# Hybrid decoder step: other tiles for the second projection part's activations

## The chip, the cores and the metric

The kernel runs on one core of a Trainium2 chip. A core has a matrix engine (TensorE, PE in the profile), three other compute engines (VectorE, DVE; ScalarE, ACT; GpSimd, POOL), a sequencer that in this kernel issues every DMA (SyncE, SP), and sixteen DMA engines that carry them. The engines run on their own, each through its instructions in a fixed order, and wait for one another through semaphores. The metric is the device time of one execution in microseconds; the median over three runs is compared.

## What is computed

The reference is one step of one layer of a decoder trunk over 1024 prompt tokens and 8 sample sequences of one token, 1032 columns in all, with 1024 channels. All of it is fp32.

```
h    = rmsnorm(x, norm_mix)
proj = h @ w_in                       # 1024 -> 3224 columns
mix  = [ S5 | mLSTM | GLA | RWKV-7 ](proj) @ w_out
x    = x + mix
h2   = rmsnorm(x, norm_ffn)
ug, uv = split(h2 @ ffn_w_up)         # 2 x 2816
x    = x + (gelu(conv3(ug)) * uv) @ ffn_w_down
y    = rmsnorm(x, norm_final)
```

The four mixers are recurrences over the tokens, 256 channels each, computed in chunks. The sample group takes one step from given states. All final states are outputs too.

## The kernel before

Activations lie transposed, channels on the 128 partitions and tokens along the free dimension, so x is eight blocks of 128 channels. The 1032 tokens are worked in two parts (`SEGS`): columns 0 to 511, and 512 to 1031 with the eight sample columns at their end (520). A matrix product in fp32 is three products in the faster fp32r form: the activation is split into a rounded part and the rest, the weight likewise, and `mm3` (L1132) adds high by high (L1139), rest by high (L1140) and high by rest (L1141) over the eight blocks. A part of 520 columns is worked as two chunks of 260, each with a PSUM buffer of its own; there are three such buffers (`g`).

The order of the program is: `win(0)`, the input projections of the first part; the first part's mixers (`SEQ0`); `win(1)`, the projections of the second part; `w_out` and `ffn` for the first part; the second part's mixers and the decoding step (`SEQ1`); `w_out` and `ffn` for the second part. That is not the order in which it runs. A planner orders each engine's instructions at build time, from its own estimates of durations: an instruction is placed when its tile is free and its inputs are there, and among those that are ready the one with the lower number goes first. `k.pr` sets these numbers: weight loads and splits (`S`) come first of all, projections, output projection and FFN (`E`) count from the same start as the mixers but have far fewer instructions ahead of them, and the matmuls of the projections (`G`) come last, so that they fill TensorE between the mixers' own.

A tile with a tag (`ga` pool, one buffer for each tag) waits until the tile before it on that tag has been read for the last time. The tags that matter here are:

- h0 to h7, 128x2x520 each: the split activations (`htile`, L1126). They are written by `split_gain` (L1189) in `win(0)`, `win(1)` and `ffn`, and by `w_out`. The last group of FFN weights also uses h0 to h3.
- xa0 to xa7: the residual x2 of the first part, from `w_out` on. Before that, xa0 holds blocks of x for `x_rstd` (L1200), xa2 a small weight and xa3 the sample columns `hd`.
- p0 to p4: gated FFN activations. Before the FFN, p0 to p2 hold every third weight (`load_w`).
- t: a ring of five tiles for everything short-lived, among it blocks of x (`load_x`, L1146), normed blocks and the evicted projections.

For `win(1)` each of the eight blocks takes this way: `load_x` brings 128x520 of x into a t tile (L1147), GpSimd multiplies it by the reciprocal norm `k.r1` into another t tile (`split_norm`, L1197), ScalarE writes the gained and rounded part into h (L1191), VectorE the rest (L1192). `k.r1` is computed earlier, by `x_rstd`, during the first part. The last projection of `win(0)` reads h0 to h7 in that order.

SyncE issues all DMAs in one queue, weight loads (L1120), x blocks (L1147), evicted projections (L1221), rows from the mixers (yD) and to them. A load that waits for its tile holds up what stands behind it.

Of the kernel before, what the change touches and what calls it, by code (L numbers as in the profile page):

```python
# [7 lines left out]
F32=mybir.dt.float32; F32R=mybir.dt.float32r; I32=mybir.dt.int32; BF16=mybir.dt.bfloat16  # L8
# [1089 lines left out]
HW=520  # L1098

W1=5  # L1100
TB=5
# [7 lines left out]
def load_w(k,src,tags=None):  # L1109

    nc=k.nc; k.wn+=1
    if tags: r=k.wp.tile([128,1024],F32,tag="wr",name="wr",bufs=k.wb[0]); h,l=[k.ga.tile([128,1024],F32R,tag=n,name=n) for n in tags]
    elif k.w3 and k.wn%3==0: r,h,l=[k.ga.tile([128,1024],t,tag=n,name=n) for n,t in (('p0',F32),('p1',F32R),('p2',F32R))]
    else: r,h,l=[k.wp.tile([128,1024],t,tag=n,name=n,bufs=b) for n,t,b in zip(('wr','wh','wl'),(F32,F32R,F32R),k.wb)]
    shp=src.shape; n=int(np.prod(shp[1:]))
    def view(t):
        v=t[:,0:n]
        return v if len(shp)==2 else v.rearrange("p (a b)->p a b",a=shp[1]) if len(shp)==3 else v.rearrange("p (c a b)->p c a b",c=shp[1],a=shp[2])
    with k.pr('S'):
        nc.sync.dma_start(out=view(r),in_=src)  # L1120
        nc.scalar.copy(h[:,0:n],r[:,0:n])  # L1121
        for c in range(0,n,256): nc.gpsimd.tensor_tensor(out=l[:,c:c+256],in0=r[:,c:c+256],in1=h[:,c:c+256].bitcast(F32),op=ALU.subtract)  # L1122
    return view(h),view(l)

def tt(k): return k.tp.tile([128,HW],F32,tag="t",name="t",bufs=k.tb)
def htile(k,i): return k.ga.tile([128,2,HW],F32R,tag="h%d"%i,name="h%d"%i)  # L1126
def gps(k,tag=None): return k.psm.tile([128,512],F32,tag=tag,name=tag,bufs=1 if tag=="mc" else 2) if tag else k.psg.tile([128,512],F32,tag="g",name="g")

def split_act(k,h,N,src):
# [13 lines left out]
def chunks(N):  # L1143
    return [(0,N)] if N<=512 else [(0,N//2),(N//2,N)]

def load_x(k,i,c0,c1):  # L1146
    t=tt(k); k.nc.sync.dma_start(out=t[:,0:c1-c0],in_=k.xT[i*128:(i+1)*128,c0:c1]); return t[:,0:c1-c0]  # L1147

class Ms:

# [38 lines left out]
def split_gain(k,N,i,x,gname):  # L1189
    h=htile(k,i); g=v1(k,gname,i)  # L1190
    k.nc.scalar.activation(out=h[:,0,0:N],in_=x,func=AF.Identity,scale=g)  # L1191
    k.nc.vector.scalar_tensor_tensor(out=h[:,1,0:N],in0=x,scalar=g,in1=h[:,0,0:N].bitcast(F32),op0=ALU.mult,op1=ALU.subtract)  # L1192
    return h

def split_norm(k,N,i,x,r,gname):

    t=tt(k)[:,0:N]; k.nc.gpsimd.tensor_tensor(out=t,in0=x,in1=r[:,0:N],op=ALU.mult)  # L1197
    return split_gain(k,N,i,t,gname)

def x_rstd(k,c0,c1):  # L1200
# [8 lines left out]
def w_in_fm(k,hr,seg,idx,w=None,tag=None):  # L1209
    nc=k.nc; c0,c1=seg; N=c1-c0; hs,r=hr  # L1210
    w=w or load_w(k,k.wfm[idx])
    dst,sc=k.fmdst[idx]
    e=tt(k); ps=[]
    for a,b in chunks(N):
        p=gps(k,tag); ps.append(p)
        mm3(k,p[:,0:b-a],w,hs,a,b)
    if r is not None: r=r.rstd()
    for (a,b),p in zip(chunks(N),ps):
        if r is None: nc.scalar.activation(out=e[:,a:b],in_=p[:,0:b-a],func=AF.Identity,scale=sc)
        else: nc.vector.scalar_tensor_tensor(out=e[:,a:b],in0=p[:,0:b-a],scalar=sc,in1=r[:,a:b],op0=ALU.mult,op1=ALU.mult)  # L1220
    nc.sync.dma_start(out=dst[:,c0:c1],in_=e[:,0:N])  # L1221
# [173 lines left out]
def build(ctx,tc,a):  # L1395
    nc=tc.nc; k=K(); k.nc=nc; k.tc=tc; k.pr=Pri(tc,PRI); tc.cur_priority=1000000
    for n in ('xT','wfm','wmv','wgv','wu','wg','wout','wup','wdn','wdl','yT'): setattr(k,n,a[n])
    k.wb=(2,2,2); k.wn=0; k.w3=True; k.tb=TB
    pool=lambda n,b=1,**kw: ctx.enter_context(tc.tile_pool(name=n,bufs=b,**kw))
    dr=pool("dr",space=DRAM)  # L1400
    D=lambda n,s: dr.tile(list(s),F32,name=n)
# [16 lines left out]
    def win(s):  # L1418
        c0,c1=SEGS[s]
        with k.pr('E'):  # L1420
            if s==0:
                m=Ms(k,c1-c0,1,"ma",2); hs=[]; xs=[]; w=[load_w(k,k.wfm[ORDER[0][1]])]
                xt=[k.mx.tile([128,n,512],F32,tag=g,name=g) for g,n in (('r_rc',4),('r_KB',2),('r_KR',2))]
                for i in range(8):
                    x=(xt[0][:,i] if i<4 else xt[1+(i-4)//2][:,i%2]); xs.append(x)
                    with k.pr('S'): nc.sync.dma_start(out=x,in_=k.xT[i*128:(i+1)*128,c0:c1])
                    if i==W1: w.append(load_w(k,k.wfm[ORDER[1][1]]))
                    hs.append(split_gain(k,c1-c0,i,xs[i],'nmix'))
                    if i==0: m.add(xs[0],True)
                for i in range(1,8): m.add(xs[i],True,nc.vector)  # L1430
                g=k.wgs=k.ga.tile([128,8,64],F32R,tag="xa2",name="wgs"); wr=k.mx.tile([128,8,24],F32,tag="r_12",name="r_12")
                nc.sync.dma_start(out=wr,in_=k.wg)
                nc.gpsimd.memset(g.rearrange("p k (u f)->p k u f",u=2)[:,:,:,24:32].bitcast(F32),0.0)
                nc.scalar.copy(g[:,:,0:24],wr)
                nc.gpsimd.tensor_tensor(out=g[:,:,32:56],in0=wr,in1=g[:,:,0:24].bitcast(F32),op=ALU.subtract)
                hr=hs,m
            else:
                w=[]; hr=[split_norm(k,c1-c0,i,load_x(k,i,c0,c1),k.r1.rstd(),'nmix') for i in range(8)],None
                m=(c1-c0)%128; k.hd=k.ga.tile([128,8,32+m],F32R,tag="xa3",name="hd")
                nc.gpsimd.memset(k.hd[:,:,m:32].bitcast(F32),0.0)  # L1440
                for i in range(8):
                    for u in range(2): nc.gpsimd.tensor_copy(k.hd[:,i,32*u:32*u+m],hr[0][i][:,u,c1-c0-m:c1-c0])
        for n,(kd,i) in enumerate(ORDER):
            with k.pr('E'):
                if kd=='fm': w_in_fm(k,hr,SEGS[s],i,w.pop(0) if w else None,{3:'mb',4:'mb',5:'mc'}.get(n) if s==0 else None)
                elif kd=='tm': w_in_tm(k,hr,SEGS[s],i)
                else: w_in_g(k,hr,SEGS[s])
                if s==0 and n==0: m.tokens()
            if s==0 and n==10: setup()
# [3 lines left out]
    def setup():  # L1453
        s5_setup(k,a['par'],a['bcv'],a['dT'],a['wglu'])
        with k.pr('E'): k.r1=x_rstd(k,*SEGS[1])
# [7 lines left out]
    def go(seq):  # L1463
        for z in seq.split(): run[z[0]](z[1:])
    win(0)
    go(SEQ0)
    win(1)
    nc.sync.dma_start(out=a['psh'],in_=rcD[:,:,1023:1024]); nc.sync.dma_start(out=a['osh'],in_=rcD[:,:,1024:1032])
    x2=[k.ga.tile([128,HW if m<2 else 512],F32,name="xa%d"%m,tag="xa%d"%m)[:,0:512] for m in range(8)]
    with k.pr('E'):  # L1470
        r=w_out(k,0,512,x2); k.w3=False; rest,end=ffn(k,0,512,x2,r)
    go(SEQ1)
    for hp in range(2):
        r=slice(hp*64,hp*64+64)
# [15 lines left out]
    x2=[xb.tile([128,HW],F32,name="xb%d"%m,tag="xb%d"%m) for m in range(8)]  # L1490
    with k.pr('E'):
        r=w_out(k,512,1032,x2,rest)
# [45 lines left out]
@with_exitstack  # L1538
def kernel(ctx: ExitStack, tc: tile.TileContext, args):
    build(ctx, tc, args)  # L1540
# [19 lines left out]
```

## Time and profile before

| what | value |
|---|---|
| median of three runs | 1469.35 us (1467.53 to 1475.34) |
| profiled execution, its own time | 1472.93 us |
| its span, first to last instruction | 1471.2 us |
| mean granted TensorE clock | 0.980 |
| PE busy | 1411.1 us, 96% of the span |
| DVE, POOL, ACT busy | 903.7, 914.8, 684.6 us |
| DMA | 179.80 MB, mean 122 GB/s |

The profile is one execution. Its page gives busy times, the span in 40 slices with the busy share in tenths, and the groups of instructions; other views give single instructions in order of time, one line's instructions, or the busy time in chosen stretches. A row such as `g<-h,wh 128*128 128x260` is a matmul that writes the PSUM tile g from h and the weight wh, with 260 columns. The bracket at the end of a row in the time line gives the idle time ahead of it and what ended that.

### The profile page before, as it was taken

The page shows a single profiled execution, that of the slowest core. Times are in us where ns is not written, and L with a number is a line of the kernel's source. Part 1 is how long each engine was busy: PE and PEld are TensorE (multiplying, and loading weights), DVE is VectorE, ACT ScalarE, POOL GpSimd, SP SyncE. Part 2 cuts the span into 40 slices and gives each one's busy share as a digit, 9 for nine tenths or more (in the row PEclk, how much of TensorE's full clock was granted, in tenths as well). Part 3 has the DMA queues.
Part 4 walks back from the last instruction along what each step waited for, and adds up shares of the span by engine and source line. Part 5 has one row for each costly group of instructions (what it writes and reads, how often), then busy time and mean ns, then how long its engine had stood idle before and what let it go on. Part 6 is the DMA issues. An engine that isn't in the chain of part 4 may idle for free.

```text
span 1471.2 us, 26807 instructions
## 1 busy us (share of the span) xinstructions
PE 1411.1 (96%) x10115; PEld 1239.2 (84%) x10115; DVE 903.7 (61%) x1979; ACT 684.6 (47%) x1151; POOL 914.8 (62%) x1154
## 2 busy tenths in 40 slices
PE   8879999999999989999899999999999999999997
PEld 6758878988999767777678778878999999999997
DVE  7988857667568956786946755455265434343434
ACT  6153454656376463766555436354443323222323
POOL 8555455546345664675754766877876757676764
PEclk9989998999999999999999999999999999999999
DMA  6455444743355523432223433353333232233332
GB/s 231 158 170 149 151 147 129 220 126 109 87 180 166 155 80 101 129 115 89 90 85 98 138 122 92 116 166 103 126 119 115 88 100 87 92 96 89 98 91 87
DMA packets 110266, 179.80 MB, mean 122 GB/s; under 512 B 33016, under 2 KB 67192, under 8 KB 110136
## 3 DMA queue, kind: packets, MB, share of 16 engines
q1 hardware_dynamic: 110136, 178.08, 39.3%
q8 instruction: 80, 1.31, 0.4%
q14 instruction: 50, 0.41, 0.1%
HBM read 148.10 MB, written 28.41 MB: 120 GB/s over the span
## 4 chain that ended last, share of the span: by engine, by line
PE 43%; DVE 4%; DMA 1%; ACT 1%; POOL 1%; issue 1%; DVEq 0%; SPq 0%; POOLq 0%; ACTq 0%
PE g L1139 14%; PE g L1141 14%; PE g L1140 13%; POOL wl L1122 1%; DVE t L1388 0%; ACT wh L1121 0%; DVE yo L1369 0%; DVE h L1192 0%; DMA DB<-d_o 0%; DMA DV<-r_KB 0%; PE g L1171 0%; DVE t L1323 0%; DVE xa L1305 0%; DMA b2a<-uD 0%; PE mb L400 0%
## 5 line engine op out<-in xcount | busy, mean ns | idle before, releaser
L1122 POOL TENSOR_TENSOR wl<-wr,wh 128x256 fp32r<-128x256 f32 x708 | 576.3, 845 | 276.5 <-ACT wh L1121 257.8
L1140 PE MATMUL g<-h,wh 128*128 128x260 f32 (+1 forms) x1536 | 493.0, 322 | 2.4 <-DVE h L1192 2.3
L1141 PE MATMUL g<-h,wl 128*128 128x260 f32 (+1 forms) x1536 | 491.9, 321 | 1.2 <-POOL wl L1122 1.2
L1139 PE MATMUL g<-h,wh 128*128 128x260 f32 (+1 forms) x1536 | 490.8, 321 | 0.2 <-ACT h L1191 0.2
L1121 ACT CAST wh<-wr 128x1024 fp32r<-128x1024 f32 x177 | 185.2, 1046 | 288.2 <-PE g L1140 146.6
L1140 PEld LDWEIGHTS g<-h,wh 128*128 128x128 f32 x1536 | 290.4, 189 | 28.6 <-DVE h L1192 5.8
L1141 PEld LDWEIGHTS g<-h,wl 128*128 128x128 f32 x1536 | 290.7, 189 | 23.9 <-POOL wl L1122 2.7
L1139 PEld LDWEIGHTS g<-h,wh 128*128 128x128 f32 x1536 | 289.4, 189 | 22.8 <-issue 0.9
L1139 PE MATMUL g<-p,wh 128*128 128x260 f32 (+1 forms) x496 | 162.6, 328 | 4.0 <-DVE xa L1305 2.3
L1141 PE MATMUL g<-p,wl 128*128 128x260 f32 (+1 forms) x496 | 162.0, 327 | 0.1
L1140 PE MATMUL g<-p,wh 128*128 128x260 f32 (+1 forms) x496 | 161.9, 327 | 0.0
L1139 PEld LDWEIGHTS g<-p,wh 128*128 128x128 f32 x496 | 94.7, 191 | 12.9 <-DVE xa L1305 2.8
L1141 PEld LDWEIGHTS g<-p,wl 128*128 128x128 f32 x496 | 94.6, 191 | 8.9 <-POOL wl L1122 0.6
L1140 PEld LDWEIGHTS g<-p,wh 128*128 128x128 f32 x496 | 94.7, 191 | 7.4 <-issue 0.2
L1122 POOL TENSOR_TENSOR p<-p,p 128x256 fp32r<-128x256 f32 x76 | 61.6, 841 | 42.9 <-ACT p L1121 34.7
L1305 DVE TENSOR_TENSOR xb<-xb,g 128x260 f32<-128x260 f32 x80 | 33.7, 424 | 60.7 <-PE g L1141 60.7
L1328 DVE TENSOR_TENSOR t<-g,r 128x260 f32<-128x260 f32 x44 | 18.6, 424 | 56.2 <-PE g L1141 51.2
L1305 DVE TENSOR_TENSOR xa<-xa,g 128x512 f32<-128x512 f32 x48 | 32.6, 681 | 32.0 <-PE g L1141 32.0
L1140 PE MATMUL g<-h,p 128*128 128x260 f32 (+1 forms) x144 | 48.9, 339 | 0.0
L1139 PE MATMUL g<-h,p 128*128 128x260 f32 (+1 forms) x144 | 48.6, 338 | 0.0
L1141 PE MATMUL g<-h,p 128*128 128x260 f32 (+1 forms) x144 | 48.6, 338 | 0.0
L1131 DVE TENSOR_TENSOR p<-t,p 128x512 fp32r<-128x512 f32 (+1 forms) x44 | 38.3, 871 | 16.1 <-ACT p L1130 15.9
(725 smaller groups left out, 2670.7 us busy)
## 6 DMA issues: line engine op xcount, KB each, us to landing
wr<-in_wup_dram SPq DMA_DIRECT2D x88, 512.0 KB
wr<-in_wfm_dram SPq DMA_DIRECT2D x27, 512.0 KB
wr<-in_wdn_dram SPq DMA_DIRECT2D x22, 512.0 KB
wr<-in_wdl_dram SPq DMA_DIRECT2D x22, 512.0 KB
wr<-in_wout_dram SPq DMA_DIRECT2D x13, 512.0 KB
p<-in_wfm_dram SPq DMA_DIRECT2D x11, 512.0 KB
t<-in_xT_dram SPq DMA_DIRECT2D x16, 260.0 KB
b4c<-B8Td SPq DMA_DIRECT2D x6, 512.0 KB
```

What stands on the lines that cost most here:

```text
L1121: nc.scalar.copy(h[:,0:n],r[:,0:n])
L1122: for c in range(0,n,256): nc.gpsimd.tensor_tensor(out=l[:,c:c+256],in0=r[:,c:c+256],in1=h[:,c:c+256].bitcast(F32),op=ALU.subtract)
L1131: k.nc.vector.tensor_tensor(out=h[:,1,0:N],in0=src,in1=h[:,0,0:N].bitcast(F32),op=ALU.subtract)
L1139: T.matmul(out,wh[:,i],a,start=i==0,stop=False)
L1140: T.matmul(out,wh[:,i],b,start=False,stop=False)
L1141: T.matmul(out,wl[:,i],a,start=False,stop=i==n-1)
L1305: V.tensor_tensor(out=x2[m][:,a:b],in0=x2[m][:,a:b],in1=p[:,0:b-a],op=ALU.add)
L1328: for (a,b),p in zip(ch,pg): V.tensor_tensor(out=g[:,2+a:2+b],in0=p[:,0:b-a],in1=r[:,a:b],op=ALU.mult)
```

## The change

`htile` takes its tag from a list, `k.home`, that the program sets ahead of each stage. In `win(0)` the list is h0 to h7 as before. For `win(1)` it is p3, p4, xa4, xa6, then h0 to h3. From then on it is h4 to h7, then h0 to h3, for the output projections and both FFN parts. `win(1)` loads its blocks of x into xa0 and xa1 in turn, and the norm is written over them, so that it takes no t tile. The last four blocks of x2 lie two by two in xa4 and xa6, which have the size of an h tile now; xa5 and xa7 are gone.

```
-def htile(k,i): return k.ga.tile([128,2,HW],F32R,tag="h%d"%i,name="h%d"%i)
+def htile(k,i): return k.ga.tile([128,2,HW],F32R,tag=k.home[i],name=k.home[i])
...
-def load_x(k,i,c0,c1):
-    t=tt(k); k.nc.sync.dma_start(out=t[:,0:c1-c0],in_=k.xT[i*128:(i+1)*128,c0:c1]); return t[:,0:c1-c0]
+def load_x(k,i,c0,c1,tag=None):
+    t=k.ga.tile([128,HW],F32,tag=tag,name="xr") if tag else tt(k)
+    k.nc.sync.dma_start(out=t[:,0:c1-c0],in_=k.xT[i*128:(i+1)*128,c0:c1]); return t[:,0:c1-c0]
...
-def split_norm(k,N,i,x,r,gname):
+def split_norm(k,N,i,x,r,gname,over=False):
-    t=tt(k)[:,0:N]; k.nc.gpsimd.tensor_tensor(out=t,in0=x,in1=r[:,0:N],op=ALU.mult)
+    t=x if over else tt(k)[:,0:N]; k.nc.gpsimd.tensor_tensor(out=t,in0=x,in1=r[:,0:N],op=ALU.mult)
...
+    k.home=['h%d'%i for i in range(8)]; k.wb=(2,2,2); k.wn=0; k.w3=True; k.tb=TB
...
-                w=[]; hr=[split_norm(k,c1-c0,i,load_x(k,i,c0,c1),k.r1.rstd(),'nmix') for i in range(8)],None
+                w=[]; hr=[split_norm(k,c1-c0,i,load_x(k,i,c0,c1,'xa%d'%(i%2)),k.r1.rstd(),'nmix',True) for i in range(8)],None
...
+    k.home=['p3','p4','xa4','xa6','h0','h1','h2','h3']
     win(1)
+    k.home=['h%d'%((i+4)%8) for i in range(8)]
...
-    x2=[k.ga.tile([128,HW if m<2 else 512],F32,name="xa%d"%m,tag="xa%d"%m)[:,0:512] for m in range(8)]
+    x2=[k.ga.tile([128,HW if m<2 else 512],F32,name="xa%d"%m,tag="xa%d"%m)[:,0:512] for m in range(4)]
+    for m in (4,6):
+        t=k.ga.tile([128,2,HW],F32,name="xa%d"%m,tag="xa%d"%m); x2+=[t[:,0,0:512],t[:,1,0:512]]
```

More of the change, by code (lines that the diff above doesn't have):

```diff
@@ L1397, in build @@
     for n in ('xT','wfm','wmv','wgv','wu','wg','wout','wup','wdn','wdl','yT'): setattr(k,n,a[n])
-    k.wb=(2,2,2); k.wn=0; k.w3=True; k.tb=TB
+    k.home=['h%d'%i for i in range(8)]; k.wb=(2,2,2); k.wn=0; k.w3=True; k.tb=TB
     pool=lambda n,b=1,**kw: ctx.enter_context(tc.tile_pool(name=n,bufs=b,**kw))
```

## The prediction

> **What bounds the kernel now.** I read the page first, then TensorE's share by stretches, then the queues of the engines around the stretch that stands out.
>
> ```profile
> span 1471.2 us, 26807 instructions
> PE 1411.1 (96%) x10115; PEld 1239.2 (84%) x10115; DVE 903.7 (61%) x1979; ACT 684.6 (47%) x1151; POOL 914.8 (62%) x1154
> PE   8879999999999989999899999999999999999997
> PEclk9989998999999999999999999999999999999999
> ```
>
> TensorE (PE) is the bound: it is busy for 96% of the span and no other engine passes 62%. All that can be won lies where it idles or runs at a reduced clock. The seventh slice, from 221 us, has PEclk at 8. The view of stretches looks into it:
>
> ```profile
> core 0: us, PE busy (x) PEld busy (x) DVE busy (x) ACT busy (x) POOL busy (x), PEclk, DMA share, GB/s
> 157.60:170.00 12.40, 12.40 (x72) 10.05 (x71) 11.35 (x29) 4.53 (x7) 8.50 (x10) 1.00 0.52 155
> 208.00:215.60 7.60, 7.60 (x39) 5.52 (x38) 2.59 (x6) 2.68 (x6) 2.19 (x4) 1.00 0.63 201
> 215.60:224.70 9.10, 4.14 (x49) 3.56 (x48) 8.02 (x14) 3.74 (x7) 6.06 (x8) 0.83 0.63 204
> 224.70:243.10 18.40, 18.40 (x144) 16.69 (x143) 17.11 (x34) 9.53 (x17) 13.62 (x23) 0.81 0.37 116
> 243.10:270.00 26.90, 26.90 (x245) 25.58 (x244) 14.29 (x37) 14.41 (x30) 11.05 (x17) 1.00 0.70 210
> ```
>
> PE is full up to 215.6 and again from 243.1. Between the two it idles 9.10-4.14 = 4.96 us, and then works 18.40 us at a mean granted clock of 0.81. The time lines of PE, POOL and SyncE's queue (SP), and the rows of the norm and the split, say what happens there:
>
> ```profile
> 208.41 0.39 PE L1139 MATMUL g<-h,wh 128*128 128x512 f32 x1
> 215.31 0.40 PE L1141 MATMUL g<-h,wl 128*128 128x512 f32 x1
> 223.73 1.11 PE L289 MATMUL ma<-r_rs,r_xa 64*64 64x64 f32 x8 [3.44 <-DVE r_rs L286]
> 224.77 0.80 PE L1139 MATMUL g<-h,wh 128*128 128x260 f32 x2
> 244.17 0.28 PE L1139 MATMUL g<-h,wh 128*128 128x260 f32 x1
> 244.29 0.28 PE L1140 MATMUL g<-h,wh 128*128 128x260 f32 x1
> L1147 SPq DMA_DIRECT2D t<-in_xT_dram x8: 327/336/464, 212.9 to 236.5; - x8
> L1197 POOL TENSOR_TENSOR t<-t,r x8: 1280/1304/1656, 219.6 to 239.2; 128x520 f32<-128x520 f32 x8
> L1191 ACT ACTIVATE h<-t,vec x8: 712/730/732, 223.7 to 240.6; 128x520 fp32r<-128x520 f32 x8
> L1192 DVE SCALAR_TENSOR_TENSOR h<-t,vec,h x8: 743/957/1628, 226.2 to 241.8; 128x520 fp32r<-128x520 f32 x8
> ```
>
> The first part's last projection reads its eight activation tiles from 208.4 to 215.7 (512 columns). The second part's eight columns of x are loaded only from 212.9, normed from 219.6, split from 223.7, and the last split starts at 241.8. Its first matmul (260 columns) is at 224.8. So the second part's operands are made after the first part has ended, and PE waits for them.
>
> **The change, part by part.** No compute instruction is added or removed: eight loads, eight norms, eight pairs of splits stay. What changes is which tile each waits for.
>
> *Tiles 0 to 3* (p3, p4, xa4, xa6) no longer wait for the first part. What they still need is r1, the second part's reciprocal norm, and a free tile for x:
>
> ```profile
> 156.95 0.64 ACT L1176 ACTIVATE r<-r 128x520 f32<-128x520 f32 x1
> L1440 POOL MEMSET hd<- x1: 292/292/292, 3.1 to 3.1; 128x192 f32 x1
> L1164 POOL TENSOR_TENSOR s<-s,xr x7: 1292/1336/2306, 35.4 to 94.8; 128x520 f32<-128x520 f32 x7
> ```
>
> r1 is there at 157.6. xa0 is free after the last sum of squares (94.8), xa1 from the start. The planner does hoist: the second part's memset, which waits for nothing, ran at 3.1 us, 210 us ahead of its neighbours in the code. So I expect four norms and split pairs from about 158 us: POOL 4 x 1.304 = 5.2, ScalarE 4 x 0.730 = 2.9, VectorE 4 x 0.957 = 3.8 us. They lie under PE's work, which has no idle time there (12.40 of 12.40); but VectorE is 11.35 of 12.40 busy, so the cover is thin. If all 3.8 us came through to PE, they would cost 3.8; if the same work, gone from 224 to 243 (VectorE 17.11 of 18.40), pays it back, nothing or a small gain. I take 0, since the total stays.
>
> *Tiles 4 to 7* (h0 to h3) come free in the order in which the last projection reads them: three matmuls of about (215.31-208.41)/23 = 0.30 us each, so from 209.3 on, one per 0.9 us. Their x sits in xa0 and xa1, normed in place. Two can wait there, normed, so tiles 4 and 5 need only ScalarE 0.73 and VectorE 0.96 and are there by about 212; VectorE is busy 2.59 of 7.60 us then. Tiles 6 and 7 need a load into the freed xa first:
>
> ```profile
> 212.91 0.46 SPq L1147 DMA_DIRECT2D t<-in_xT_dram  x1
> 219.66 0.33 SPq L1120 DMA_DIRECT2D wr<-in_wfm_dram  x1
> 227.67 9.14 SPq L1147 DMA_DIRECT2D t<-in_xT_dram  x4
> 248.56 0.33 SPq L1120 DMA_DIRECT2D wr<-in_wfm_dram  x1
> 233.32 1.31 POOL L1197 TENSOR_TENSOR t<-t,r 128x520 f32<-128x520 f32 x1 [1.66 <-DMA t<-in_xT_dram]
> ```
>
> Four loads took 9.14 us of SP's queue, 2.3 each. With one load, norm and split pair (2.3+1.3+0.7+1.0 = 5.3) tile 6 is ready near 217.5 and tile 7 near 219. By then PE has tiles 0 to 5 for the first projection's two halves: 6 x 3 x 2 = 36 matmuls, 0.12 us apart (244.17 to 244.29), 4.3 us from 215.7 to 220.0, beside the mixers' own matmuls. The bubble left is 0 by this, and 3.4 us if the load is as late as the one that held POOL at 233.3; I take 0.5.
>
> *The gain.* The idle 4.96 us go. The clock: 18.40 x (1-0.81) = 3.50 us. Sum 8.46. If the bubble left stays short, both go together; less 0.5 that is 8.0.
>
> The clock term rests on rows: 0.83 and 0.81 granted after PE's 3.44 us wait, 1.00 before and after. The Trainium skill (TensorE: Matmul & The Clock Gate, section "What's actually happening") says the clock falls to half after about one idle window of 3.4 us and comes back after as long of work; the trace agrees with its 3.44 us. By that rule a bubble of 0.5 us costs no clock, so the 3.50 goes whole or not at all.
>
> *Smaller edits.* Column 1's load into xa1 waits for nothing and may go out at the start: 260 KB, which at the 204 GB/s of the stretch quoted take 1.3 us; between 0 (a queue with room) and 1.3 (all ahead of the first operands); I take 0. The norm in place drops eight t tiles from the shared ring of five, which eases the projections' evictions: no gain counted. The last four x2 halves share xa4 and xa6, which the second part now reads to its end; x2 is written after that, so the wait is over before it starts. FFN and output projection rotate to h4 first: the same matmuls. At the very end the last weights go into h0 to h3, now the later four tiles, and so come free 12 matmuls x 0.12 = 1.4 us later, under a whole group of 8 x 2 x 12 matmuls (23 us): 0.
>
> *What is late next.* The output projection after the second part:
>
> ```profile
> 456.95 0.39 SPq L583 DMA_DIRECT2D yD<-b2a  x1
> 827.92 2.42 DMA yD<-b2a
> 466.13 2.68 SPq L1277 DMA_DIRECT2D t<-yD  x4
> 470.91 0.62 ACT L1130 CAST h<-t 128x512 fp32r<-128x512 f32 x1 [0.51 <-DMA t<-yD]
> 469.11 0.28 PE L1141 MATMUL g<-h,wl 128*128 128x260 f32 x1
> 473.20 0.48 PE L1139 MATMUL g<-h,p 128*128 128x512 f32 x1
> ```
>
> The second part would end at 469.4-8.0 = 461.4. The last mixer's rows are stored at 456.95, land 2.42 later (an equal store), and from load to first matmul pass 473.20-466.13 = 7.1: 466.4. The gap becomes 5.0 instead of 3.8 us, with mixer matmuls in it either way. That takes 0 to 1.2; I take 0, because h4 to h7 are free by then and the loads need not queue.
>
> After that nothing stands in the way of the gain: the last decoding mixer stores its rows at 976, and the second output projection's weights go out at 1002.
>
> ```profile
> 975.99 0.38 SPq L1047 DMA_DIRECT2D yD<-d_g  x1
> 1002.33 11.59 SPq L1120 DMA_DIRECT2D wr<-in_wout_dram  x3
> ```
>
> That is 26 us of slack against 8.
>
> **The sum.** The profiled execution took 1472.93 (span 1471.2 and 1.7 around it), 3.6 over the median of 1469.35, inside the runs shown. On its own time: 1472.93-8.0 = 1464.9; carried to the median, 1469.35-8.0 = 1461.4. The open costs (3.8 early splits, 2.9 more of bubble, 1.3, 1.2) do not all fall together; with about half of their 9.2, 4.6, the forecast's own range is 1457 to 1466, its lower end from the third rival's gap filled.
>
> **The rivals.**
>
> *Only the first four help.* If tiles 4 to 7 come as late as now, PE gains what tiles 0 to 3 feed: three PSUM buffers x 4 x 3 matmuls x 0.12 = 4.3 us: 1465.0. For it: two x tiles only, and loads that queue behind others on SP. Against it: tiles 4 and 5 need no load at that time.
>
> *The gain stops at the output projection.* VectorE at 92% from 157.6 to 170 gets 3.8 us more and POOL 5.2, both ahead of the mixers by the planner's priorities. If the mixers before the output projection are late by 5.2, their rows land at 464.6 and the first matmul is at 471.6 instead of 473.2: a gain of 1.6, 1467.7. Rows for it: the same split took 743 to 1628 ns, the norm 1280 to 1656. The Trainium skill (SBUF — State Buffer, section "SBUF: two separate sides") says that VectorE with two SBUF inputs and a reading GpSimd lock each other out of one port for a whole instruction; the spread agrees, and by that rule the early pairs stretch instead of fitting in. Against this rival: 224 to 243 gets lighter by the same amount.
>
> *More than forecast.* The output projection's gap of 3.8 us closes too, since its first four tiles are free early: 8.46+3.8 = 12.3, 1457.1. It needs the last mixer some 12 us earlier, and only VectorE's lighter load speaks for that.
>
> *Slower: loads that wait at SP's head.* With two x tiles, six loads wait for a split of the load two before. At 2.3 us each that is 13.7 us in which SP issues nothing else, moved from a stretch where PE had no operands into 158 to 216, where PE is full and the weights (L1120) and the mixers' loads queue behind. It decides once a wait outlasts the three weight sets held; uncovered, 13.7 plus 3.5 of clock less 8.0: 1469.35+9.2 = 1478.6. Against it: the planner places a load where it expects the tile to be free.
>
> **How the numbers follow.** Forecast 0.50, first four only 0.16, stopped at the output projection 0.08, more 0.12, slower 0.14. Changes under 0.5%, 7.3 us here, can't be told from none: faster is under 1462.0, slower over 1476.7. The forecast lies on the edge: 0.32 of its 0.50 below 1462.0. Faster: 0.32+0.12+0.03 (from the first rival) = 0.47. Slower: 0.14. Same: 0.39. The range holds all but the last rival: from 1457.1 and 1467.7 it reaches outward by 3 and 6 us, about what the runs shown lie below and above their median (1467.53 and 1475.34, 1.8 and 6.0): 1454 to 1474.
>
> **What would show it.** Right: four norms (L1197, now x<-x) near 158 to 180; first 260-column matmul within 1 us of the last 512-column one; granted clock 1.00 through 216 to 243; the second part's end near 461. Wrong: splits of tiles 4 to 7 still after 220 (first rival); y's loads waiting near 459 with PE idle behind (second); x loads of several us on SP before 208 with PE idle (slower).

## The result, and the profile after

The changed kernel takes 1495.24 us (median of 4 runs, 1489.45 to 1498.19) against 1470.32 us (median of 4, 1467.53 to 1475.34) for the kernel before on the same chip. The ratio is 1.0158 with a 95% interval of 1.0138 to 1.0178: slower by 1.6%, where 1461.4 and a gain were forecast. The profiled execution is the fastest of the four, 1489.45 us with a span of 1487.6 against 1471.2, so the traces show 16.4 us of the loss. Two executions in the experiments below lie far from all others of their kernel (1696.96 us in e10, 3120.18 us in e11); they are in the medians given there, but not in the ratios.

The page's span, its busy line for TensorE (PE) and its 40 slices, of the kernel after:

```profile
span 1487.6 us, 26798 instructions
PE 1423.3 (96%) x10115; PEld 1243.5 (84%) x10115; DVE 928.8 (62%) x1979; ACT 681.1 (46%) x1151; POOL 925.9 (62%) x1154
PE   8699999999999989999999999999999999999997
PEclk9899999999999989999999999999999999999999
```

The 8 of the clock in the slice from 221 us is gone. The five engines have the same counts of instructions as before. VectorE (DVE) is busy 25.1 us longer than before (903.7) though it does the same work. The view of stretches, at the places that the prediction read and with the columns shown there:

```profile
157.60:170.00 12.40, 12.40 (x72) 10.04 (x71) 11.60 (x20) 4.96 (x7) 11.78 (x15) 1.00 0.50 155
208.00:215.60 7.60, 7.60 (x63) 6.15 (x63) 3.57 (x4) 6.30 (x11) 7.46 (x10) 1.00 0.41 124
215.60:224.70 9.10, 9.10 (x70) 8.01 (x69) 6.71 (x9) 5.15 (x9) 8.68 (x12) 1.00 0.61 188
224.70:243.10 18.40, 18.40 (x171) 17.10 (x172) 11.88 (x35) 9.53 (x20) 6.74 (x13) 1.00 0.49 174
```

PE is busy 9.10 of 9.10 us where it idled 4.96, and the granted clock is 1.00 where it was 0.83 and 0.81. The rows of the norm (now L1198) and of VectorE's half of the split (now L1193):

```profile
L1198 POOL TENSOR_TENSOR xr<-xr,r x8: 1288/1540/1941, 160.0 to 218.5; 128x520 f32<-128x520 f32 x8
L1193 DVE SCALAR_TENSOR_TENSOR h<-xr,vec,h x4: 760/1181/1233, 212.7 to 223.5; 128x520 fp32r<-128x520 f32 x4
L1193 DVE SCALAR_TENSOR_TENSOR p<-xr,vec,p x2: 1195/1216/1237, 166.6 to 167.7; 128x520 fp32r<-128x520 f32 x2
L1193 DVE SCALAR_TENSOR_TENSOR xa<-xr,vec,xa x2: 1103/1104/1105, 174.7 to 177.8; 128x520 fp32r<-128x520 f32 x2
```

Four tiles are ready by 179, the other four by 224.7. So the tiles come early, as intended. What that cost is first seen on the chain of RWKV's first chunk. VectorE's time line, before and then after: one step of the forward substitution (L247), its end (the transpose L248), and the first of four state updates (L296).

```profile
169.99 0.21 DVE L247 TENSOR_TENSOR ma<-ma,r 128x50 f32<-128x50 f32 x1
193.25 0.66 DVE L248 STREAM_TRANSPOSE r<-ma 128x256 f32<-128x256 f32 x1
218.16 0.90 DVE L296 TENSOR_TENSOR r_S<-r_S,r 128x256 f32<-128x256 f32 x1
```

```profile
178.87 0.20 DVE L247 TENSOR_TENSOR ma<-ma,r 128x50 f32<-128x50 f32 x1
200.41 0.70 DVE L248 STREAM_TRANSPOSE r<-ma 128x256 f32<-128x256 f32 x1
230.38 0.42 DVE L296 TENSOR_TENSOR r_S<-r_S,r 128x256 f32<-128x256 f32 x1
```

The same step is 8.9 us late behind the four early splits, the substitution ends 7.2 us late, and the first state update is 12.2 us late. The other 5.0 came on between 200 and 230, and PE's time line shows a part of it. In the kernel before, around the bubble, the matmuls of one state update (L281 and L284, L289, L293):

```profile
214.42 0.39 PE L284 MATMUL ma<-r_KB,r_rc 128*64 128x64 f32 x4
215.63 0.68 PE L289 MATMUL ma<-r_rs,r_xa 64*64 64x64 f32 x8
216.95 0.71 PE L293 MATMUL ma<-r_KB,r 128*128 128x128 f32 x4 [0.64 <-DVE r_KB L290]
```

and in the kernel after, with the two parts' projections:

```profile
217.40 0.39 PE L1141 MATMUL g<-h,wl 128*128 128x512 f32 x1
217.62 0.28 PE L1139 MATMUL g<-p,wh 128*128 128x260 f32 x1
219.85 0.40 PE L284 MATMUL ma<-r_KB,r_rc 128*64 128x64 f32 x4
223.98 0.68 PE L289 MATMUL ma<-r_rs,r_xa 64*64 64x64 f32 x8
227.80 0.61 PE L293 MATMUL ma<-r_KB,r 128*128 128x128 f32 x4
```

The first 260-column matmul starts 0.22 us after the last 512-column one: no bubble. But from L284 to L293 RWKV's step now takes 7.95 us (227.80 - 219.85) instead of 2.53 (216.95 - 214.42). VectorE has a share in it: its copy behind L284 (L286) starts at 222.35, 2.1 us after L284 has ended, since L448 and L468 stand ahead of it.

The lateness goes on. The last matmul of the second part's projections (469.11 before), the first one of the output projection (473.20 before), the last mixer's rows for the output projection of the first part (SyncE's queue; 456.95 before), the y loads that follow them, and the weights of the second output projection (1002.33 before):

```profile
468.52 0.28 PE L1141 MATMUL g<-h,wl 128*128 128x260 f32 x1
469.32 0.40 PE L1139 MATMUL g<-h,p 128*128 128x512 f32 x1
472.16 0.37 SPq L583 DMA_DIRECT2D yD<-b2a  x1
475.74 2.13 SPq L1278 DMA_DIRECT2D t<-yD  x4
1017.85 0.33 SPq L1120 DMA_DIRECT2D wr<-in_wout_dram  x1
```

The second part's projections end at 468.8, 0.6 us earlier than before and not 8.0: the gain at 216 is spent by then. The output projection starts 3.9 us earlier, on the mixers that are done, but the last mixer's rows are 15.2 us late, the second weights 15.5, the span 16.4. On PE the gain at 216 is given back in small waits. Of the stretches of 50 us, two of before and the same two of after:

```profile
250.00:300.00 50.00, 50.00 (x450) 45.58 (x451) 32.30 (x67) 32.94 (x65) 25.86 (x38) 1.00 0.68 208
450.00:500.00 50.00, 49.26 (x368) 42.23 (x367) 44.59 (x103) 29.41 (x54) 27.86 (x34) 1.00 0.55 171
```

```profile
250.00:300.00 50.00, 48.04 (x436) 42.92 (x437) 28.76 (x61) 22.78 (x48) 20.68 (x35) 0.97 0.54 163
450.00:500.00 50.00, 47.23 (x308) 40.30 (x307) 38.64 (x79) 29.96 (x62) 20.19 (x31) 0.93 0.46 144
```

and four of the waits in PE's time line after (the last number is the idle time, then who ended it):

```profile
177.95 0.69 PE L400 MATMUL mb<-b4f 128*64 128x64 f32 x16 [2.39 <-DVE r L246]
290.87 0.82 PE L112 MATMUL ma<-r,lora 96*128 96x256 f32 x4 [1.96 <-DVE r L108]
372.18 1.22 PE L257 MATMUL ma<-r_KB,r_rc 32*32 32x32 f32 x32 [2.13 <-ACT r_KB L249]
477.86 0.50 PE L1139 MATMUL g<-h,p 128*128 128x512 f32 x1 [1.92 <-ACT h L1130]
```

Three of the four stand at a mixer's matmul that is late, the fourth at the output projection. Each engine works through a fixed order, so the projections' matmuls behind such an instruction can't fill the wait. In the table each pair is PE's idle time and the time lost to the clock, busy x (1 - granted clock), in us, summed from stretches of 50 us:

| stretch | before | after |
|---|---|---|
| 150 to 200 | 0.0 + 0.0 | 2.7 + 1.4 |
| 200 to 250 | 5.0 + 4.5 | 0.0 + 0.0 |
| 250 to 450 | 1.5 + 0.0 | 5.0 + 2.9 |
| 450 to 500 | 0.7 + 0.0 | 2.8 + 3.3 |
| 500 to 600 | 7.1 + 4.7 | 7.1 + 8.3 |
| 600 to 900 | 11.2 + 2.7 | 12.0 + 2.8 |

The 9.5 us between 200 and 250 are won; 20.4 are lost elsewhere. The balance is 10.9 of the 16.4 us. The other 5.5 is time in which PE counts as busy, which I can't place.

### The profile page after: what moved, and what is told of

Same layout as the page of the kernel before. It is cut to its first block, busy times and chain, and to the rows that moved or that the text cites. A ratio compares the mean times of both kernels' runs of the same rounds, so it can differ in the third digit from the quotient of the medians.

```text
span 1487.6 us, 26798 instructions
## 1 busy us (share of the span) xinstructions
PE 1423.3 (96%) x10115; PEld 1243.5 (84%) x10115; DVE 928.8 (62%) x1979; ACT 681.1 (46%) x1151; POOL 925.9 (62%) x1154
## 4 chain that ended last, share of the span: by engine, by line
PE 64%; DVE 16%; POOL 6%; ACT 5%; issue 4%; DMA 4%; SPq 0%; DVEq 0%; POOLq 0%; ACTq 0%
PE g L1140 17%; PE g L1139 17%; PE g L1141 17%; POOL wl L1122 4%; PE ma L213 1%; ACT wh L1121 1%; POOL p L1122 1%; DMA yD<-b2a 1%; POOL s L1165 1%; PE g L1238 1%; PE g L1240 1%; PE g L1241 1%; PE mb L829 1%; PE ma L281 1%; DVE t L126 1%
## 5 line engine op out<-in xcount | busy, mean ns | idle before, releaser
L1140 PE MATMUL g<-h,wh 128*128 128x260 f32 (+1 forms) x1424 | 461.9, 325 | 3.1 <-DVE h L1193 3.0
L1141 PE MATMUL g<-h,wl 128*128 128x260 f32 (+1 forms) x1424 | 460.8, 324 | 0.8 <-POOL wl L1122 0.6
L1139 PE MATMUL g<-h,wh 128*128 128x260 f32 (+1 forms) x1424 | 459.9, 324 | 1.4 <-ACT h L1192 0.8
L1140 PEld LDWEIGHTS g<-h,wh 128*128 128x128 f32 x1424 | 269.5, 189 | 27.9 <-DVE h L1193 5.7
L1141 PEld LDWEIGHTS g<-h,wl 128*128 128x128 f32 x1424 | 270.1, 190 | 23.9 <-POOL wl L1122 2.5
L1139 PEld LDWEIGHTS g<-h,wh 128*128 128x128 f32 x1424 | 269.4, 189 | 24.1 <-issue 1.2
L1139 PE MATMUL g<-p,wh 128*128 128x260 f32 (+1 forms) x552 | 178.3, 323 | 5.6 <-DVE xa L1306 3.6
L1140 PE MATMUL g<-p,wh 128*128 128x260 f32 (+1 forms) x552 | 178.1, 323 | 0.0
L1141 PE MATMUL g<-p,wl 128*128 128x260 f32 (+1 forms) x552 | 176.9, 321 | 0.9 <-POOL wl L1122 0.9
L1139 PEld LDWEIGHTS g<-p,wh 128*128 128x128 f32 x552 | 104.3, 189 | 16.0 <-DVE xa L1306 5.5
L1140 PEld LDWEIGHTS g<-p,wh 128*128 128x128 f32 x552 | 104.6, 189 | 8.2 <-issue 0.7
L1341 DVE TENSOR_TENSOR t<-t,g 128x260 f32<-128x260 f32 x44 | 16.7, 421 | 48.3 <-POOL t L1340 48.3
L1318 DVE SCALAR_TENSOR_TENSOR t<-g,vec,t 128x511 f32<-128x511 f32 (+1 forms) x44 | 32.6, 741 | 19.4 <-ACT t L1317 19.1
L1338 ACT ACTIVATE t<-t 128x520 f32<-128x520 f32 x22 | 14.1, 639 | 61.3 <-DVE t L1334 61.3
```

The source lines that it names most:

```text
L1139: T.matmul(out,wh[:,i],a,start=i==0,stop=False)
L1140: T.matmul(out,wh[:,i],b,start=False,stop=False)
L1141: T.matmul(out,wl[:,i],a,start=False,stop=i==n-1)
L1318: for o,n in ((1,'cw1'),(2,'cw0')): V.scalar_tensor_tensor(out=acc[:,o:N],in0=p[:,0:N-o],scalar=v1(k,n,j),in1=acc[:,o:N],op0=ALU.mult,op1= ...
L1341: for (a,b),q in zip(ch,pv): V.tensor_tensor(out=acc[:,a:b],in0=acc[:,a:b],in1=q[:,0:b-a],op=ALU.mult)
```

## The experiments

Each is compared with the kernel before on the same chip. "First L296" is RWKV's first state update, 218.2 us before and 230.4 after. Single times come from one profiled execution each, and among the kernels that lose nothing L248 itself moves by up to 3.7 us. The edits are shown shortened.

**Which part of the edit.** Four kernels: the changed kernel with its loads, norms and splits numbered behind all mixers; the changed kernel with the late way of x (the t ring); x in xa0 and xa1 but the splits in h0 to h7; the rotation alone.

```
e1  + with k.pr('L'): hr=[split_norm(...)]        # L=3000000
e2  - load_x(k,i,c0,c1,'xa%d'%(i%2)), ..., True   + load_x(k,i,c0,c1), ...
e3  - k.home=['p3','p4','xa4','xa6','h0',...]     # and x2 as before
e4  as e2, without the p3, p4, xa4, xa6 homes
```

> The changed kernel with one edit: the second part's x loads, norms and splits get a number behind all the mixers' instructions, so the planner places them only where an engine has nothing of the mixers ready. Setback theory (the early norms and splits went ahead of the first RWKV chunk, whose first state update moved from 218 to 230 us, and the rows that the output projection waits for moved from 457 to 472): the first state update is back at 216 to 222, those rows are stored by 460, and the time is 1458 to 1470 us. Reshuffle theory (any edit that moves tiles gives another order everywhere, and the loss is not tied to these splits): 1482 to 1500 us as in the changed kernel. Rotation theory (the loss comes from the output projection and FFN taking h4 first and x2 in pairs): 1482 to 1498 us, with the RWKV step back at 218.

> The changed kernel, but x goes through the ring t again and is not normed in place; the tile lists and the x2 pairs stay. In the kernel before, the ring let the first x load go at 212.9 us. Setback theory: no split before 212, RWKV's first state update at 216 to 222, and the time is 1462 to 1473 us. Reshuffle theory: 1480 us or more. Rotation theory: 1480 us or more, lost after 470 us.

> Only x in xa0 and xa1, normed in place; the activations are in h0 to h7 throughout and x2 in eight tiles, as before. At most two norms can run early, no split. Setback theory: the first state update is late by 0 to 3 us, and the time is 1466 to 1476 us. Reshuffle theory: 1480 us or more. Rotation theory: 1466 to 1473 us.

> Only the list h4 to h7, h0 to h3 from the output projection on, and x2's last four halves in two tiles; the second part's projection is as before. Setback theory: 1466 to 1473 us, as the kernel before. Reshuffle theory: 1480 us or more. Rotation theory: 1482 to 1498 us.

Measured: e1 1494.45 us, ratio 1.0163 (1.0132 to 1.0193); e2 1471.74, 1.0004 (0.9988 to 1.0019); e3 1474.33, 1.0019 (1.0003 to 1.0035); e4 1471.14, 0.9993 (0.9977 to 1.0009). In e1 the early splits stayed at 167 to 179 in spite of the number, so e1 took nothing away and decides nothing. The rotation, the shared x2 tiles and x in xa0 and xa1 each cost nothing or nearly nothing. It takes early loads and early homes together, that is, early splits. In e3 the first 260-column matmul comes at 216.03, with no gap behind the first part, and 18 of them run between L284 and L293, which takes 4.1 us; but the bubble only moved: PE waits 0.99 and 2.90 us at the second state update, and nothing is won. So an early first matmul alone costs next to nothing.

**The splits without the projections, and the other way round.** e5 is the changed kernel with r1 held until the first part's last token-major projection is evicted (near 200 us). e6 is the kernel before, late way and all, with four loads, norms and split pairs added at 160 to 180 into tiles that nothing reads (x2 stays in pairs in xa4 and xa6, which costs nothing in e4; so in e8 to e10). e7 has two early tiles instead of four. e8 has the added loads and norms of e6, without the splits.

```
e5  + nc.scalar.activation(out=r1,in_=r1,func=AF.Identity,scale=k.late[:,0:1])   # late: ones
e6  + k.home=['p3','p4','xa4','xa6']
    + for i in range(4): split_norm(k,c1-c0,i,load_x(k,i,c0,c1,'xa%d'%(i%2)),k.r1.rstd(),'nmix',True)
e7  - k.home=['p3','p4','xa4','xa6','h0','h1','h2','h3']
    + k.home=['p3','p4','h0','h1','h2','h3','h4','h5']      # afterwards h6, h7, h0 to h5
e8  as e6, with only the load and gpsimd.tensor_tensor(x*r1) for each
```

> The changed kernel, but r1 is multiplied in place by a tile of ones that is made from the first eviction of the last projection of the first part (one more ScalarE operation of about 0.64 us, one tiny VectorE operation), so that the four early norms and splits can start only near 200 us, behind RWKV's first chunk, where VectorE is busy 4 of 12 us. Theory A (setback: the early splits push RWKV's chain back on a full VectorE, and the loss is passed down): first state update (L296) back near 218 to 224 instead of 230, time 1460 to 1471. Theory B (filler: the projections that start early, without the bubble, take from the mixers the time on TensorE that the bubble gave them): the early splits' place does not matter, L296 still at 226 or later, time 1482 or more.

> The kernel before, with its late loads, norms and splits unchanged, and four more loads, norms and split pairs ahead, in tiles that nothing reads (p3, p4, xa4, xa6): added work whose results are unused. Theory A: they run at 160 to 180, L296 first at 228 to 232, time 1485 to 1500, though the projections start as late as before. Theory B: no loss beyond the work itself, 1470 to 1476.

> The changed kernel with only two of the eight tiles early (p3, p4), the other six from h0 to h5. Theory A: half of the splits ahead of RWKV's chain, so about half of the delay: L296 first at 222 to 227, time 1474 to 1486. Theory B: the bubble is mostly closed too, since two tiles feed the first matmuls, so nearly the whole loss: 1486 to 1495.

> As e6, but the four unused early pieces are loads and norms on POOL alone, without ScalarE's and VectorE's splits. If the delay comes from VectorE's own 4.6 us of splits, most of it is gone: L296 at 218 to 222, 1469 to 1476. If it comes from POOL's norms stretching VectorE's two-input operations, or holding POOL's own work for the mixers, most of it stays: L296 at 225 or later, 1480 or more.

Measured: e5 1497.72 us, 1.0177 (1.0148 to 1.0206), first L296 at 228.0; e6 1493.70, 1.0151 (1.0127 to 1.0175), at 224.8; e7 1495.94, 1.0170 (1.0133 to 1.0207), at 231.2; e8 1473.00, 1.0008 (0.9990 to 1.0026), at 220.6. VectorE's time line in e6, where nothing needs the early splits:

```profile
167.75 2.35 DVE L1193 SCALAR_TENSOR_TENSOR p<-xr,vec,p 128x520 fp32r<-128x520 f32 x2
176.28 1.10 DVE L1193 SCALAR_TENSOR_TENSOR xa<-xr,vec,xa 128x520 fp32r<-128x520 f32 x1
179.41 1.10 DVE L1193 SCALAR_TENSOR_TENSOR xa<-xr,vec,xa 128x520 fp32r<-128x520 f32 x1
180.44 0.20 DVE L247 TENSOR_TENSOR ma<-ma,r 128x50 f32<-128x50 f32 x1
```

Against 169.99 the step is 10.5 us late, for 4.55 us of splits, and L248 is 7.8 late. The first L296 is less late than expected (224.8, not 228), but e6 loses nearly as much as the change though its projections start as late as before: the early splits alone are enough (theory A). The loads and norms without them cost nothing (e8), so neither SyncE's queue nor GpSimd is to blame. But e5 fell out against A: with the splits held back to 200, L248 is at 194.6, only 1.4 us late, and the loss is whole. And e7 shows that A is not in proportion: two splits cost what four do. A second cause was needed.

**ScalarE, size, order, GpSimd.** e9 is e8 with ScalarE's halves of the splits; e10 is e6 with norm and split 130 columns wide; e11 is the kernel before with each late VectorE split in two pieces, which changes VectorE's planned order in some 400 places; e12 is the changed kernel with the early rest halves made by ScalarE and GpSimd.

```
e9   as e8, + nc.scalar.activation(out=h[:,0],in_=tx,func=AF.Identity,scale=g)
e10  - split_norm(k,c1-c0,i,load_x(...),...)   + split_norm(k,130,i,load_x(...)[:,0:130],...)
e11  + for lo,hi in ((0,260),(260,N)): vector.scalar_tensor_tensor(out=h[:,1,lo:hi],...)
e12  + scalar.activation(out=x,in_=x,func=AF.Identity,scale=g)
     + gpsimd.tensor_tensor(out=h[:,1],in0=x,in1=h[:,0],op=ALU.subtract)      # i<4
```

> The kernel before with four more unused early loads, norms and ScalarE halves of the split, but no VectorE halves. Theory A (VectorE's time in RWKV's first chunk is what costs): no loss, first state update (L296) at 218 to 221, 1469 to 1476. If ScalarE's 2.9 us ahead of the mixers cost as well: L296 at 223 or later, 1478 or more.

> As the run with four unused early pieces (the loads still whole), but norm and split only 130 of the 520 columns wide: about a quarter of the work on VectorE, at the same place. Theory A, in proportion: VectorE loses about 1.2 us instead of 4.6, first L296 at 219 to 223, 1470 to 1478. Theory D (the loss comes from the four VectorE instructions standing between the chain's steps, whatever their width, since RWKV's chain is one of short steps): L296 at 226 or later, 1485 or more.

> The kernel before, with the VectorE half of the eight late splits in two instructions of 260 columns each (8 instructions more, under 1 us in all, where TensorE waits for them). It changes the planned order of VectorE from the late splits on in some 400 of its 1691 instructions, but puts nothing ahead of RWKV's first chunk. Theory A: L296 at 217 to 221, 1467 to 1476. Theory C (any new order from the planner costs those 23 us): 1485 or more.

> The changed kernel, but the rest half of the early four tiles is made by ScalarE (the gain, in place, 0.7 us each) and GpSimd (a subtraction, 1.3 us each) instead of VectorE. Theory A: VectorE's chain keeps its time, first L296 at 218 to 223, the bubble at 216 is still closed, and the time is 1460 to 1472. If the projections that start early are what costs (theory B): L296 at 226 or later or later mixers' steps late by 10 us or more, 1480 or more.

Measured: e9 1472.41 us, 1.0012 (0.9999 to 1.0024), first L296 at 218.2; e10 1474.64, 1.0024 (1.0009 to 1.0040), at 220.6; e11 1477.37, 1.0042 (1.0019 to 1.0066), at 220.7; e12 1490.53, 1.0129 (1.0103 to 1.0156), at 228.2. ScalarE's part costs nothing that can be measured; a quarter of VectorE's costs 0.2% where the whole costs 1.5%. A new order costs a little by itself (e11: 0.4%, 1.4 us above the range expected of it), not 20 us. e12 keeps the early splits off VectorE and still loses 1.3%. Its L248 is at 196.4, 3.2 late, but as late in e2 and e8, which lose nothing (196.4 and 196.5), and its L296 at 228.2, 10.1 late: the second cause sits between 196 and 228, where the bubble was.

**The bubble itself, and lateness by itself.** e13 is the kernel before with 36 matmuls whose result nothing reads, ready near 217. e14 and e15 are the kernel before with ten and twenty copies of RWKV's matrix onto itself on ScalarE ahead of L248, in the first chunk only.

```
e13  + A.activation(out=k.fz,in_=e[:,0:260],func=AF.Identity)      # at that eviction
     + for n in range(36): nc.tensor.matmul(p[:,0:260],k.fz[:,0:128],k.fz,start=True,stop=True)
e14  + if q==0: for _ in range(10): A.copy(X,X)
e15  + if q==0: for _ in range(20): A.copy(X,X)
```

> The kernel before with 36 matmuls of 128x260 whose result nothing reads (about 4.3 us of TensorE), which become ready when the first part's last token-major projection is evicted and so can fill the bubble at 216 to 224. Added work; VectorE and GpSimd get none, ScalarE one operation. If the bubble is idle time of nobody (as the prediction had it), they fit in: L296 at 218 to 221, 1467 to 1476. Theory B (in the bubble RWKV's state updates follow each other at once, and work put there stands between them): they stand between its steps, first or second L296 late by 3 us or more against 218 and 228, and the time is up by more than the 4.3 us, 1478 or more.

> The kernel before, with RWKV's first chunk held by ten copies of its matrix onto itself on ScalarE (10 x about 0.35 us) between the substitution chain and its transpose. Added work, none of it on VectorE, GpSimd or TensorE. Theory E (the mixers' chain sets the end as much as TensorE does, so that lateness in the first chunk is passed down): first L296 at 221 to 224, 1474 to 1482. If a late first chunk is caught up again: 1468 to 1474.

> As the run with ten copies, with twenty (about 7 us). Theory E: first L296 at 225 to 228, 1482 to 1495, the losses of the changed kernel without its splits and without its early projections. If lateness is caught up: 1468 to 1474.

Measured: e13 1487.87 us, 1.0112 (1.0074 to 1.0150), first L296 at 227.2; e14 1473.22, 1.0024 (1.0012 to 1.0037), at 220.4; e15 1484.37, 1.0089 (1.0063 to 1.0115), at 229.5. PE's time line in e13 (L1442 is the added matmul):

```profile
217.31 2.30 PE L1442 MATMUL g<-fz 128*128 128x260 f32 x18
219.54 0.67 PE L289 MATMUL ma<-r_rs,r_xa 64*64 64x64 f32 x8
220.15 2.41 PE L1442 MATMUL g<-fz 128*128 128x260 f32 x18
222.39 0.60 PE L293 MATMUL ma<-r_KB,r 128*128 128x128 f32 x4
```

4.7 us of matmuls laid in the "idle" bubble cost 18.1 us (1487.87 - 1469.74). They stand between L284, L289 and L293 as the early projections do in the changed kernel. They also hold one of the three `g` buffers, a side effect that no run separates. And e15 shows that lateness needs no such company: a chain held up on ScalarE, with no work added on PE, VectorE or GpSimd, loses 14.6 us. In e14 L248 is 4.8 us late, L296 only 2.2, and the end 3.5, which is in the range expected if lateness is caught up.

**The other direction.** e16 is the kernel before with the rest halves of its eight late splits on ScalarE and GpSimd, e17 with the last four of them; e18 is the changed kernel with all eight there.

```
e16, e17  split_gain of before as in e12, for all eight late tiles or for i>3
e18       as e12, for all eight
```

> The kernel before, with the rest half of the eight late splits made by ScalarE (the gain in place, 0.7 us) and GpSimd (a subtraction, 1.3 us) instead of VectorE (1.0 us each, at 226 to 242, where RWKV's four state updates run). Theory E, turned round: the chain is freed of 7.7 us of VectorE's work, the fourth L296 comes before 254, at 246 to 251, and the time falls below that of the kernel before: 1455 to 1466. Against it: GpSimd now makes norm and rest (2.6 us a tile against 2.3 of SyncE's load), the operands come later, and the bubble grows: 1470 to 1480.

> As e16, for the last four of the eight only. Theory E: half of the relief, the fourth L296 at 250 to 253, 1460 to 1469. Against it: 1470 or more, as GpSimd's late pieces hold back the first weights' splits.

> The changed kernel with the rest halves of all eight tiles made by ScalarE and GpSimd: VectorE has no work for them at all, at 160 to 180 or at 212 to 224. If VectorE's splits between RWKV's steps are what makes the closed bubble cost: first L296 at 218 to 222, the bubble stays closed, 1458 to 1468, better than both kernels. Theory B (the projections' matmuls between RWKV's steps on TensorE suffice): first L296 at 223 or later and 1478 or more.

Measured: e16 1470.35 us, 0.9994 (0.9976 to 1.0011); e17 1475.93, 1.0038 (1.0023 to 1.0052); e18 1483.60, 1.0097 (1.0075 to 1.0120). In e16 the fourth L296 comes at 248.1 instead of 254.0, as expected, and against the expected gain nothing is won: PE's idle time from 200 to 300 is 6.1 us against 5.0, so an earlier chain alone does not fill it. In e17 it comes at 253.2 and 0.4% is lost; why is open. In e18 the rest halves are off VectorE altogether, and PE and VectorE show:

```profile
218.38 0.40 PE L284 MATMUL ma<-r_KB,r_rc 128*64 128x64 f32 x4
221.98 0.68 PE L289 MATMUL ma<-r_rs,r_xa 64*64 64x64 f32 x8
225.56 0.61 PE L293 MATMUL ma<-r_KB,r 128*128 128x128 f32 x4
```

```profile
229.96 0.43 DVE L296 TENSOR_TENSOR r_S<-r_S,r 128x256 f32<-128x256 f32 x1
```

From L284 to L293 it takes 7.18 us, close to the 7.95 of the changed kernel, with projection matmuls between. The last leg, from L293 to L296, is 4.4 us against 1.2 before (218.16 - 216.95): VectorE's scans for the gates (L469 and L473, 223.8 to 227.4), which ran after the first L296 in the kernel before (220.0 to 223.2), are now planned ahead of it. So with the bubble closed the planner lays other work between RWKV's steps on both engines (theory B, and more than it said).

All eighteen in one order, by the first L296: at 221.3 or earlier (e2, e3, e4, e8 to e11, e14, e16, e17) the ratio is at most 1.0042; at 224.8 or later (e5 to e7, e12, e13, e15, e18, e1 and the change) it is at least 1.0089. There is no case of a first L296 that late without a loss of 0.9% or more. The lateness at L248 (193.25 before) and the way from there to the first L296 keep the two causes apart, in us:

| kernels | L248 late by | L248 to first L296 | ratio |
|---|---|---|---|
| before | 0 | 24.9 | 1 |
| e2 to e4, e8 to e11, e16, e17 | -1.1 to 3.7 | 23.6 to 25.6 | 0.9993 to 1.0042 |
| e14 | 4.8 | 22.3 | 1.0024 |
| e6, e15 | 7.8, 14.5 | 23.8, 21.8 | 1.0151, 1.0089 |
| e5, e13 | 1.4, 1.7 | 33.4, 32.3 | 1.0177, 1.0112 |
| e12, e18 | 3.2, 3.5 | 31.8, 33.2 | 1.0129, 1.0097 |
| e7 | 6.1 | 31.8 | 1.0170 |
| changed kernel, e1 | 7.2, 7.8 | 30.0, 30.2 | 1.0158, 1.0163 |

Either a late L248 with the bubble open (e6, e15) or a longer way with L248 on time (e5, e13) is enough; the changed kernel has both.

## Why the prediction was wrong, point by point

- **What bounds the kernel.** "All that can be won lies where it idles or runs at a reduced clock" may hold for what can be won, but says nothing of what can be lost. PE at 96% hid a second chain, the mixers': made 5.9 us earlier at its fourth update (e16) it gains nothing, made 11.3 us later at its first (e15) it costs 14.6. The two fit a chain about as long as PE's work; that is an inference, no run measures its length.
- **Four norms near 158 to 180, the last 512 columns and the first 260 together, clock 1.00.** These three came: norms at 160.0 to 172.6, 0.22 us, 1.00. The gain of 8.46 is 9.5 in the table. The fourth sign, the second part's end near 461, failed: it ended at 468.8.
- **"I take 0, since the total stays"** for the early splits. This is the first step that failed. The stretch quoted had VectorE 11.35 of 12.40 busy and RWKV's substitution in it, a chain of steps of 0.2 us each that gives way to every split and to what the planner moves with it. The four splits took 4.6 us, above the bound of 3.8, and other VectorE operations beside them 3.4 us more than before (last section); the chain was late by 8.9 at that step and by 7.2 at its end. e6 puts the price of such splits at 22.8 us, where 3.8 was the most allowed for. That the same work is gone from 224 to 243 pays nothing back: e16 frees VectorE there and gains nothing.
- **"The idle 4.96 us go"** at their full worth. This is the second. PE's idle time there was the time in which RWKV's state updates followed each other at once (2.53 us from L284 to L293). Filled, by the projections or by matmuls that nothing reads, the way from L248 to the first L296 is 5.1 to 8.5 us longer (the table above), and PE waits later: e13 loses 18.1 us where 0 was assumed.
- **Bubble left over 0.5, edits at 0.** The bubble left is 0. The rotation and x2's tiles cost nothing, as taken (e4, e2); xa1's early load and the norm in place cost 0.2% (e3, 1.0003 to 1.0035).
- **"What is late next."** The rows were expected at 456.95 as before; they came at 472.16. "26 us of slack" at the end was no help: the second output projection's weights go out 15.5 us late, with PE's backlog.
- **The rivals.** "The gain stops at the output projection" named the right engine and the right kind of lateness, but sized it at 5.2 us where it is 15.2, left out the part that the closed bubble adds, and let it end at the output projection, though it is passed on to the end. Its remark that the early pairs would stretch was right (1.1 to 1.2 us for a split instead of 0.96). The slower rival, loads at SyncE's head, is not what happened, though its time was nearest: SyncE waited 6.1 us in all for these loads from 155 to 216, 1.5 at most at once, where 13.7 were feared, and e8 issues four early loads at 1.0008. "Only the first four help" fell: tiles 4 to 7 were split at 212.7 to 224.7, the last two after 220 and later than forecast, but PE had no gap.

What stays open: how the loss at the end divides between the two causes in the changed kernel (each alone costs 13 to 27 us, e18 to e5, both together 25, so they don't add); why the loss at the end can be over three times the lateness of the first update (22.8 us for 6.6 in e6) and follows it so loosely; and the 5.5 us of PE's busy time. No version here is faster than the kernel before.

## What to carry to other kernels

Idle time on the bounding engine may be the place where a latency chain of another part runs undisturbed; before counting it as gain, look which small instructions stand in it and what they feed. "The total stays" is no price for work that is moved: look whose chain it lands in, and test it by adding the same work there with its result unused. When a second chain may be about as long as the bounding engine's work, price what a change does to it too.

## What the runs showed of the hardware

A short wait on TensorE can cost more than itself. The view of stretches around the wait of 1.96 us that ended at 290.87 in the changed kernel (PE's busy time and, behind POOL's, its granted clock):

```profile
286.00:288.90 2.90, 2.90 (x25) 2.71 (x23) 2.84 (x6) 0.81 (x2) 2.36 (x4) 1.00 0.26 96
288.90:290.90 2.00, 0.04 (x2) 0.06 (x1) 1.94 (x4) 0.00 (x0) 1.60 (x3) 1.00 0.16 26
290.90:292.50 1.60, 1.60 (x12) 1.21 (x12) 1.58 (x6) 0.00 (x0) 0.70 (x5) 0.63 0.74 135
292.50:294.00 1.50, 1.50 (x15) 1.00 (x12) 0.00 (x1) 1.40 (x3) 0.00 (x0) 0.50 0.13 8
294.00:296.00 2.00, 2.00 (x22) 1.09 (x20) 1.27 (x2) 0.58 (x1) 0.00 (x0) 0.82 0.12 7
```

PE was full before it, and after a wait of 1.96 us the clock was down to 0.50: 0.59 + 0.75 + 0.36 = 1.7 us more, each stretch's busy time by what is missing to 1.00. The waits that ended at 177.95 (2.39 us) and 372.18 (2.13 us) were followed by a clock of 0.50 as well, the kernel before's at 353.11 (1.48 us) by 1.00. The Trainium skill (TensorE: Matmul & The Clock Gate, section "What's actually happening"), which the prediction used, has the clock fall after an idle window of about 3.4 us; these waits are shorter, and the measurement decides. No single limit comes out of the two profiles, before and after: of their 28 waits of 1.4 us or more, the five up to 1.68 us left the clock at 1.00 and the twelve from 2.13 us on were followed by 0.50, but between them both happened (1.72 us, ended at 1114.30 before: 0.50; 2.04 us, ended at 543.22 before: 1.00). The prediction's "comes back after as long of work" is not seen at its bubble either: after 3.44 us of waiting PE was full, and the clock stayed near 0.50 for about 8 us, until 232. So one bubble broken into several of 2 us need be no saving, and this is part of why lateness came back larger than it was.

Some of VectorE's operations with two SBUF inputs became longer in the changed kernel beside the early norms, those with a PSUM input shown here did not. The groups of VectorE from 150 to 200 us, busy us and mean ns behind the bar, before and then after:

```profile
L1220 DVE SCALAR_TENSOR_TENSOR t<-g,r 128x512 f32<-128x512 f32 x5 | 3.4, 684 | 0.0
L387 DVE TENSOR_TENSOR b4e<-b4e,b4a 128x256 f32<-128x256 f32 x4 | 2.2, 553 | 0.0
```

```profile
L1221 DVE SCALAR_TENSOR_TENSOR t<-g,r 128x512 f32<-128x512 f32 x5 | 3.4, 682 | 0.0
L387 DVE TENSOR_TENSOR b4e<-b4e,b4a 128x256 f32<-128x256 f32 x4 | 4.4, 1106 | 0.0
```

GpSimd was busy 33.20 of these 50 us instead of 23.74. The operation of two SBUF tiles doubles from 553 to 1106 ns; the eviction of g, which is in PSUM, stays at 684 and 682. With their neighbours of the same kind (L387 into b4f 744 to 914 ns, L386 into b4f 1007 to 1226, into b4e 822 to 834) they took 3.4 us more. The Trainium skill (SBUF — State Buffer, section "SBUF: two separate sides") says that a VectorE operation with two SBUF inputs and a GpSimd operation that reads SBUF lock each other out of a shared port for a whole instruction, and the two rows agree with it. By this count, an estimate, the 3.4 us are a part of the first cause: splits (4.6) and longer neighbours together are 8.0, and the substitution, which began 1.0 us earlier than before, ended 7.2 late. It isn't needed for the loss: in e5 and e13 the same group is at 552 and 553 ns.
